# SBUF addresses of the activations moved relative to their weights in every dense product, and the scheduling clock's price of a matmul set to columns plus 17 cycles

## The chip, the cores and the metric

One core of one Trainium2 chip runs the whole program in one launch. The metric is the device time of that launch in microseconds. TensorE (PE in the profile) does the matrix products, VectorE (DVE) and ScalarE (ACT) the elementwise work, GpSimd (POOL) a few fills and some DMA issues, and the SyncE queue (SP) issues most DMAs. The working memory, SBUF, has 128 partitions; a tile has the same byte address in each of them, and an address below is that byte address within a partition.

## The reference, cut to what matters

One layer over 256 latent tokens and 256 context tokens, model width 2048:

```python
z = einsum('bld,dc->blc', h, w_in)            # latent and context
y_s5 = s5_mixer(z[..., :1024], ...)           # complex diagonal state space, scans
y_rw = rwkv_mixer(z_rw mixed with neighbours) # sequential state update, 16 heads, 2 directions
glu = gelu(y_s5) @ s5_glu_w
merged = gate1 * glu_a * sigmoid(glu_b) + gate2 * (y_rw @ rw_proj)
h = h + g1 * (merged @ w_o)
z = modulate(rms_norm(h, norm2_w), sh2, sc2) @ ffn_w13
h = h + g2 * ((silu(z[..., :D_FF]) * z[..., D_FF:]) @ ffn_w2)   # D_FF = 5632
out = rms_norm(h, norm_f)
```

The modulation vectors (shifts, scales and gates) are six blocks of `silu(c) @ ada_w + ada_b`. Everything is fp32.

## The kernel before, in words

**The dense products.** Six weight matrices are multiplied by activations that lie in SBUF as [128, k, tokens]: `win` (activations `hc` for context and `hl` for latent tokens), `glu` (`gl`), `proj` (`yr`), `wo` (`mg`), `w13` (`h2`) and `w2` (`hid`). Weights come from HBM in halves of eight 128x128 tiles (512 KB). ScalarE rounds a half to the reduced fp32 type (`hi`), VectorE makes the rest (`lo` = weight minus `hi`); the activations have been split in the same way into two tiles (names ending in 0 and 1). `Dense.step` then issues, for each 128x128 weight tile, three matmuls into one PSUM accumulator: `hi` with activation 0, `hi` with activation 1, `lo` with activation 0. Each has its own weight load of 128 columns and then moves 256 columns of activations, or 258 in `w13`, where two columns carry the shift. The counts of such matmuls are `win` 1248 with `hc` and 3216 with `hl`, `glu` 768, `proj` 384, `wo` 768, `w13` 4224 and `w2` 2112.

**The order of the work.** Background generators (the S5 and RWKV branches, evacuations, weight preparation) and dense steps are interleaved by `Kernel.drive`. It keeps a rough clock of every engine (`Clock`): `Clock.cost` gives each instruction a price, and `drive` emits a dense step where the picked background step would have to wait on that clock. The order of emission in each engine's queue is fixed by this when the program is built; nothing of it runs on the chip.

**The stages.** A start-up (modulation vectors, norms) runs to about 124 us of the span. Then come the `win` columns used by both token sets (to about 485), the latent-only and gate columns (to about 831) beside S5 and RWKV, the modulation matrix `adaR` as raw fp32 matmuls beside RWKV (about 835 to 1160), `glu` (to 1312), `proj` (to 1370), `wo` (to 1460), `w13` (to 1970) and `w2` (to 2219). The last three have nothing but evacuations and weight preparation beside them, and during `w13` the generator `mod_late`, which makes the last modulation block on VectorE: 32 products of [128, 1024] weights with the row `cbs`, loaded over the GpSimd queue.

**Where tiles lie.** Pools are opened and closed like a stack. A left pool is placed upward from the end of the last left pool, the first of them at 4224; a right pool downward from the start of the last right one. The pools `hr` that hold `hi` and `lo` consist of tiles of 4096 bytes, a weight tile is 512 bytes of one, and one k of the activations is 1024 bytes (1088 in `h2`). So a product's activations stand at one distance from their weights by 512, whichever tile and ring slot is used, and only in `h2` the distance moves with k. Adding up the tile sizes of the pools gives this for the kernel before, all by 512:

| product | activations | weights | distance |
|---|---|---|---|
| win, hc | 0 | 448 | 64 |
| win, hl | 448 | 448 | 0 |
| glu, gl | 128 | 128 | 0 |
| proj, yr | 128 | 448 | 192 |
| wo, mg | 0 | 448 | 64 |
| w13, h2 | 128 + 64 k | 448 | 192 + 64 k |
| w2, hid | 0 | 448 | 64 |

The `glu` weights are in left pools, all other weights in right pools at the top of SBUF.

Of the kernel before, what the change touches and what calls it, by code (L numbers as in the profile page):

```python
# [8 lines left out]
F32 = mybir.dt.float32  # L9
# [8 lines left out]
P = 128  # L18
# [160 lines left out]
class Clock:  # L179
# [41 lines left out]
    def cost(self, eng, op, out, a, k):  # L221
        n = 1
        for d in out.shape[1:]:
            n *= d
        if eng == "tensor":
            if op == "transpose":
                return 0.055 if a[1].shape[0] <= 64 else 0.108
            self.mms += 1
            lhs = k["lhsT"]
            m = lhs.shape[-1]  # L230
            if lhs.dtype == F32R:

                return max(n / 2400 + 0.002, 0.12)

            return (4 * max(n, m) if max(n, m) > 64 else 3 * n) / 2400 + 0.002
        if eng == "vector":
            src = a[1] if len(a) > 1 else k.get("in_")
            if op in ("tensor_copy", "tensor_scalar"):
                return 0.07 + n / (960 if "ps" in src.tensor.name[:2] else 1400)
            if op == "reciprocal":  # L240
                return 0.07 + 6 * n / 960
            return 0.07 + n / 960
        if eng == "scalar":
            c = (0.05 if a[1].tensor.name[:2] == "ps" else 0.1) + n / 1200
            for q in ("bias", "scale"):
                if _aps(k.get(q)) is not None:
                    c += 0.09
            c += self.table_load(a[2])
            return c
        return 0.1 + n / 1000  # L250
# [319 lines left out]
class Kernel:  # L570
# [16 lines left out]
    def pool(self, name, bufs=1, side=None, space=None):  # L587
# [4 lines left out]
            kw["space"] = space  # L592
        return Pool(self.tc.tile_pool(**kw), self.clk, bufs)

    def wide(self, pool, n, tag, name=None, bufs=None):

        return pool.tile([P, -(-n // 16) * 16], F32, tag=tag, name=name or tag, bufs=bufs)[:, 0:n]
# [10 lines left out]
    def run(self):  # L608
        nc, tc, A = self.nc, self.tc, self.A
        es = ExitStack()  # L610
        with es:
            cpool = es.enter_context(self.pool("cpool"))
            dr = es.enter_context(self.pool("dr", space=DRAM))
            self.free_banks, self.held = [], {}
            self.add_banks(es, 4)
            self.cpool = cpool

            edge = es.enter_context(self.pool("edge", side="right"))
            edge.tile([P, 8], F32, tag="edge", name="edge")
            self.cst = self.wide(cpool, NCST, "cst")  # L620
            pp = cpool.tile([P, NPP + 29], F32, tag="pp", name="pp")
            self.pp, self.omu, self.tiny = pp[:, 0:NPP], pp[:, NPP:NPP + 27], pp[:, NPP + 27:]
            nc.gpsimd.dma_start(self.pp, A["pp"])
            nc.gpsimd.dma_start(self.cst, A["cst"])
            self.ada = cpool.tile([P, 96, 2], F32, tag="ada", name="ada")
            self.arow = cpool.tile([P, T], F32, tag="arow", name="arow")
            nc.gpsimd.memset(self.arow, 0.0)
            self.sc = cpool.tile([P, KT, 2], F32, tag="sc", name="sc")
            nc.vector.tensor_scalar(self.omu, self.pc("mu", 0, 27), -1.0, 1.0, op0=ALU.mult, op1=ALU.add)
            self.hka = cpool.tile([P, 2, 8], F32, tag="hka", name="hka")  # L630
            nc.vector.tensor_scalar(self.hka[:, 0], self.pc("ka", 0, 8), 0.5, None, op0=ALU.mult)
            nc.vector.tensor_scalar(self.hka[:, 1], self.pc("ka", 0, 8), -0.5, 1.0, op0=ALU.mult, op1=ALU.add)
            self.hwa = cpool.tile([P, 2, 16], F32, tag="hwa", name="hwa")
            nc.vector.tensor_scalar(self.hwa[:, 0], self.pc("w0", 0, 16), 0.5, None, op0=ALU.mult)
            nc.vector.tensor_scalar(self.hwa[:, 1], self.pc("a0", 0, 16), 0.5, None, op0=ALU.mult)
            nc.vector.memset(self.tiny[:, 0:1], 1e-12)
            nc.vector.memset(self.tiny[:, 1:2], GN_EPS)
            self.A2 = cpool.tile([P, 16], F32, tag="A2", name="A2")
            self.zc = ExitStack()
            self.zcp = zcp = self.zc.enter_context(self.pool("zcp"))  # L640
            self.wad = [zcp.tile([P, 2, T], F32, tag=f"wad{e}", name=f"wad{e}") for e in range(2)]
            self.sgd = zcp.tile([P, T], F32, tag="sgd", name="sgd")
            self.S = [zcp.tile([P, 2, 2, 64], F32, tag=f"S{e}", name=f"S{e}") for e in range(4)]


            self.d_u = dr.tile([1024, 4, 2, 64], F32, tag="d_u", name="d_u")
            self.d_kvr = [dr.tile([P, 512], F32, tag=f"d_kvr{i}", name=f"d_kvr{i}") for i in range(24)]
            self.d_kk = [dr.tile([P, 512], F32, tag=f"d_kk{j}", name=f"d_kk{j}") for j in range(8)]
            self.d_gate = dr.tile([2, P, 16, T], F32, tag="d_gate", name="d_gate")
            self.d_ma = dr.tile([P, 16, T], F32, tag="d_ma", name="d_ma")  # L650
            self.d_win = dr.tile([4, P, 4096], F32, tag="d_win", name="d_win")
            self.d_wout = dr.tile([2, 4, P, 1024], F32, tag="d_wout", name="d_wout")
            self.d_yr = dr.tile([P, 8, T], F32, tag="d_yr", name="d_yr")
            self.d_y = dr.tile([1024, 4, 64], F32, tag="d_y", name="d_y")

            self.flags = Flags(self.clk)
            self.bgs = []
            self.make_jobs()
            self.spawn(self.dense.evacuate(), "evac", self.PRD)
            self.spawn(self.dense.preps(), "prep", self.PRD)  # L660
            self.body()
# [141 lines left out]
    def e_mod(self, q, acc):  # L803


        nc = self.nc
        yield "scalar", acc
        ar = self.arow[:, q % 2 * P:q % 2 * P + P]
        gs = [slice(32 * g, 32 * g + 16) for g in range(4)]
        for g in gs:  # L810
            nc.scalar.activation(ar[g], acc[g], AF.Copy)
        self.dense.drop()
        yield "tensor:1", self.arow
        tp = self.bank([P, 16], f"psmod{q}")
        for g in gs:
            nc.tensor.matmul(tp, lhsT=ar, rhs=self.cs("ident")[:, g], start=(g.start == 0), stop=(g.start == 96))
        f = 32 + 16 * q
        yield "vector", tp
        nc.vector.tensor_tensor(self.ada[:, f:f + 16, 0], tp, self.pc("adab", f, f + 16), op=ALU.add)
        self.free(tp)  # L820
        if q == 2:
            nc.vector.scalar_tensor_tensor(self.A2, self.ada[:, 64:80, 0], 1.0, self.pc("n2", 0, 16), op0=ALU.add, op1=ALU.mult)

    def mod_late(self, pool):

        nc = self.nc
        cbs = pool.tile([P, D], F32, tag="cbs", name="cbs")
        raw = pool.tile([P, 16, 2], F32, tag="adr", name="adr")
        row = self.A["crow"][0:1, :]
        nc.gpsimd.dma_start(cbs, bass.AP(row.tensor, row.offset, [[0, P], [1, D]]))  # L830
        yield "scalar", cbs
# [1 line left out]
        ws = []  # L833

        def load(i):
            if i < 32:
                ws.append(pool.tile([P, 1024], F32, tag="adw", name=f"adg{i}", bufs=2))
                nc.gpsimd.dma_start(ws[i], self.A["adaG"][i // 2][:, 1024 * (i % 2):1024 * (i % 2) + 1024])

        load(0)  # L840
        load(1)
        for i in range(32):
            yield lambda: self.dense.pos >= self.n_wo + 8 + 4 * i
            self.clk.mark = 0.0
            self.after(ws[i])
            yield "vector"
            f, e = i // 2, i % 2
            nc.vector.scalar_tensor_tensor(ws[i], ws[i], 1.0, cbs[:, 1024 * e:1024 * e + 1024], op0=ALU.mult, op1=ALU.mult,
                                           accum_out=raw[:, f, e:e + 1])
            load(i + 2)  # L850
        o = self.ada[:, 80:96, 0]
        nc.vector.tensor_tensor(o, raw[:, :, 0], raw[:, :, 1], op=ALU.add)
        nc.vector.tensor_tensor(o, o, self.pc("adab", 80, 96), op=ALU.add)

# [1433 lines left out]
    def body(self):  # L2288
# [4 lines left out]
        d = self.dense  # L2293
        d.open(0, self.n_win, side="right")
        hl = ExitStack()
        self.hlp = hl.enter_context(self.pool("hlp", side="right"))
        gx = ExitStack()
        self.gp = gx.enter_context(self.pool("gp", side="right"))
# [47 lines left out]
        d.open(self.n_mod, self.n_glu, ahead=1)  # L2346
        d.top_up()
        glx = ExitStack()
        glp = glx.enter_context(self.pool("glp"))
        self.gates = {}  # L2350
        self.spawn(self.load_gl(glp), "gl")
# [38 lines left out]
        self.drive(self.n_proj, drain=False)  # L2390
        tail.close()
        h2p = rest.enter_context(self.pool("h2p", side="right"))
        self.h2 = [h2p.tile([P, KT, T + 16], F32R, tag=f"h2{e}", name=f"h2{e}")[:, :, 0:T + 2] for e in range(2)]
        self.shifts()
        self.drive(self.n_wo, drain=False)
        mgx.close()
# [70 lines left out]
```

## Time and profile before

| | |
|---|---|
| median of 3 runs | 2234.84 us (2229.05 to 2236.33) |
| the profiled execution | 2237.06 us, of which its instructions span 2235.3 us |
| mean granted TensorE clock | 0.944 of full speed |
| HBM read, written | 399.77 MB, 31.98 MB: 193 GB/s over the span |

Times below are microseconds from the first instruction of the profiled execution. PE is the matmuls and PEld the weight loads, which overlap them. A matmul's record lasts longer than the step from one start to the next, since matmuls are pipelined; the step is what the sums use. PEclk is the granted clock as a share of full speed (1.00 is 2.4 GHz, 0.5 is 1.2 GHz). All instructions are recorded by one helper and bear its line, L315, so groups are told apart by their tiles: `psacc` is the accumulator of the dense products (and of `adaR`), and in the tile names of the profile numbers are left out, so that `h` is `h2`.

### The profile page before, as it was taken

What the parts mean: (1) busy time and instruction counts of PE and PEld (TensorE: products, weight loads), DVE (VectorE), ACT (ScalarE), POOL (GpSimd) and SP (SyncE); (2) the same over time, 40 slices, a digit from 0 to 9 for tenths busy, and PEclk for the clock granted to TensorE, in tenths of its full rate; (3) what the DMA queues carried; (4) which work ended last, traced back from release to release, by engine and by line L of the source; (5) the groups of instructions that cost most, each with busy time, mean ns of one, the idle gap of its engine ahead of it and who ended that gap; (6) DMA issues with size and microseconds to landing.
All of it is one profiled execution on the core that took longest, in us unless ns stands there. A gap on an engine that the chain in (4) does not pass through costs nothing.

```text
span 2235.3 us, 48212 instructions
## 1 busy us (share of the span) xinstructions
PE 2091.9 (94%) x19780; PEld 1888.3 (84%) x19780; DVE 1472.7 (66%) x2879; ACT 1103.5 (49%) x1897; POOL 156.7 (7%) x325
## 2 busy tenths in 40 slices
PE   7999999999998998787879879999999999999997
PEld 2279999999897886464648879999999999999997
DVE  2788847899836775787675647656666665554444
ACT  2245455334647767383747535554444444444333
POOL 0001110000101102020011110000000000000000
PEclk9999999999998988586869999999999999999998
DMA  9945556356664445747454386557777775555553
GB/s 366 345 165 185 185 180 207 121 156 211 223 182 158 133 137 168 230 139 231 128 172 142 123 301 206 186 186 232 227 230 230 228 219 185 184 188 185 186 188 132
DMA packets 155980, 434.90 MB, mean 195 GB/s; under 512 B 26480, under 2 KB 39792, under 8 KB 154864
## 3 DMA queue, kind: packets, MB, share of 16 engines
q1 hardware_dynamic: 130192, 360.76, 49.7%
q0 software_dynamic: 18080, 58.48, 7.6%
q10 hardware_dynamic: 7488, 12.59, 1.5%
q8 instruction: 155, 2.54, 0.5%
q14 instruction: 65, 0.53, 0.1%
HBM read 399.77 MB, written 31.98 MB: 193 GB/s over the span
## 4 chain that ended last, share of the span: by engine, by line
PE 68%; DVE 12%; ACT 9%; DMA 8%; issue 3%; SPq 0%; POOL 0%; ACTq 0%; DVEq 0%; POOLq 0%
PE psacc L315 56%; DVE lo L315 4%; DMA w<-in_adaR_dram 4%; PE adacc L315 2%; DMA w<-in_glu_dram 2%; ACT hi L315 1%; PE psyp L315 1%; DVE r L315 1%; PE psbu L315 1%; ACT L315 1%; DMA ad<-in_adaP_dram 1%; ACT AQh L315 1%; PE psss L315 1%; DVE zs L315 1%; ACT SV1h L315 1%
## 5 line engine op out<-in xcount | busy, mean ns | idle before, releaser
L315 DVE TENSOR_TENSOR lo<-w,hi 128x1024 fp32r<-128x1024 f32 x478 | 584.5, 1224 | 412.4 <-ACT hi L315 399.9
L315 ACT ACTIVATE hi<-w 128x1024 fp32r<-128x1024 f32 x478 | 505.9, 1059 | 689.8 <-PE psacc L315 554.6
L315 PE MATMUL psacc<-h,hi 128*128 128x258 f32 x2816 | 507.5, 283 | 1.1 <-ACT hi L315 1.1
L315 PEld LDWEIGHTS psacc<-h,hi 128*128 128x128 f32 x2816 | 436.6, 190 | 1.4 <-ACT hi L315 1.4
L315 PE MATMUL psacc<-hl,hi 128*128 128x256 f32 x2144 | 415.9, 288 | 0.0
L315 PE MATMUL psacc<-h,lo 128*128 128x258 f32 x1408 | 398.1, 283 | 0.8 <-DVE lo L315 0.8
L315 PEld LDWEIGHTS psacc<-hl,hi 128*128 128x128 f32 x2144 | 336.3, 192 | 7.8 <-issue 7.2
L315 PE MATMUL psacc<-hl,lo 128*128 128x256 f32 x1072 | 306.6, 286 | 1.4 <-DVE lo L315 1.4
L315 PEld LDWEIGHTS psacc<-h,lo 128*128 128x128 f32 x1408 | 268.0, 190 | 1.0 <-DVE lo L315 1.0
L315 PE MATMUL psacc<-hid,hi 128*128 128x256 f32 x1408 | 248.8, 280 | 0.0
L315 PEld LDWEIGHTS psacc<-hid,hi 128*128 128x128 f32 x1408 | 214.9, 188 | 0.0
L315 PEld LDWEIGHTS psacc<-hl,lo 128*128 128x128 f32 x1072 | 206.3, 192 | 1.8 <-DVE lo L315 1.8
L315 PE MATMUL psacc<-hid,lo 128*128 128x256 f32 x704 | 196.4, 279 | 0.0
L315 PE MATMUL psacc<-hc,hi 128*128 128x256 f32 x832 | 172.0, 288 | 0.0
L315 PE MATMUL psacc<-w,scp 128*16 128x128 f32 x1536 | 95.8, 357 | 54.1 <-DMA w<-in_adaR_dram 52.8
L315 PEld LDWEIGHTS psacc<-hc,hi 128*128 128x128 f32 x832 | 129.7, 191 | 2.8 <-issue 1.9
L315 PEld LDWEIGHTS psacc<-hid,lo 128*128 128x128 f32 x704 | 131.6, 187 | 0.0
L315 PEld LDWEIGHTS psacc<-w,scp 128*16 128x16 f32 x1536 | 32.2, 106 | 108.9 <-DMA w<-in_adaR_dram 99.5
L315 PE MATMUL psacc<-hc,lo 128*128 128x256 f32 x416 | 116.7, 280 | 0.0
L315 PE MATMUL adacc<-ad,sc 128*2 128x512 f32 x192 | 92.0, 633 | 15.4 <-ACT sc L315 7.8
L315 PE MATMUL psacc<-gl,hi 128*128 128x256 f32 x512 | 98.7, 293 | 1.7 <-ACT hi L315 1.6
L315 PE MATMUL psacc<-mg,hi 128*128 128x256 f32 x512 | 90.5, 280 | 0.0
(371 smaller groups left out, 3398.3 us busy)
## 6 DMA issues: line engine op xcount, KB each, us to landing
w<-in_w_dram SPq DMA_DIRECT2D x264, 512.0 KB, 3.7
w<-in_win_dram SPq DMA_DIRECT2D x134, 512.0 KB, 3.9
w<-in_adaR_dram SPq DMA_DIRECT2D x192, 256.0 KB, 3.4
ad<-in_adaP_dram SPq DMA_DIRECT2D x48, 512.0 KB, 6.4
w<-in_glu_dram SPq DMA_DIRECT2D x32, 512.0 KB, 3.7
adg<-in_adaG_dram POOLq DMA_DIRECT2D x32, 512.0 KB, 5.3
w<-in_wo_dram SPq DMA_DIRECT2D x32, 512.0 KB, 4.2
ad<-in_adaD_dram SPq DMA_DIRECT2D x16, 512.0 KB, 7.3
```

Source lines behind the costliest of these rows:

```text
L315: return f(*a, **k)
```

## The change

Pool sizes and two row lengths change so that tiles move; the price of a dense matmul in the rough clock changes; and `mod_late` works in 64 pieces of 512 columns with three buffers, where it had 32 pieces of 1024 with two. `gap` opens a pool whose one tile nothing uses. `arow`, the row buffer of `e_mod`, had two halves used in turn and has one.

```diff
-                return max(n / 2400 + 0.002, 0.12)
+                return n / 2400 + 0.007
...
+    def gap(self, es, n, side=None):
+        es.enter_context(self.pool("gap", side=side)).tile([P, n], F32, tag="gap", name="gap")
...
-            self.arow = cpool.tile([P, T], F32, tag="arow", name="arow")
+            self.arow = cpool.tile([P, P], F32, tag="arow", name="arow")
...
             self.A2 = cpool.tile([P, 16], F32, tag="A2", name="A2")
+            cpool.tile([P, 32], F32, tag="fill", name="fill")
...
-        ar = self.arow[:, q % 2 * P:q % 2 * P + P]
+        ar = self.arow
...
-        raw = pool.tile([P, 16, 2], F32, tag="adr", name="adr")
+        raw = pool.tile([P, 16, 4], F32, tag="adr", name="adr")
...
-            if i < 32:
-                ws.append(pool.tile([P, 1024], F32, tag="adw", name=f"adg{i}", bufs=2))
-                nc.gpsimd.dma_start(ws[i], self.A["adaG"][i // 2][:, 1024 * (i % 2):1024 * (i % 2) + 1024])
+            if i < 64:
+                ws.append(pool.tile([P, 512], F32, tag="adw", name=f"adg{i}", bufs=3))
+                nc.gpsimd.dma_start(ws[i], self.A["adaG"][i // 4][:, 512 * (i % 4):512 * (i % 4) + 512])
...
-        for i in range(32):
-            yield lambda: self.dense.pos >= self.n_wo + 8 + 4 * i
+        for i in range(64):
+            yield lambda: self.dense.pos >= self.n_wo + 8 + 2 * i
...
+        nc.vector.tensor_tensor(raw[:, :, 0:2], raw[:, :, 0:2], raw[:, :, 2:4], op=ALU.add)
...
         hl = ExitStack()
+        self.gap(hl, 80, "right")
         self.hlp = hl.enter_context(self.pool("hlp", side="right"))
...
         glx = ExitStack()
+        self.gap(glx, 48)
         glp = glx.enter_context(self.pool("glp"))
...
-        self.h2 = [h2p.tile([P, KT, T + 16], F32R, tag=f"h2{e}", name=f"h2{e}")[:, :, 0:T + 2] for e in range(2)]
+        self.h2 = [h2p.tile([P, KT, T + 128], F32R, tag=f"h2{e}", name=f"h2{e}")[:, :, 0:T + 2] for e in range(2)]
```

## Rows read from the trace of the kernel before

**Rows 1.** The page: busy time and share of the span of each engine.
```profile
PE 2091.9 (94%) x19780; PEld 1888.3 (84%) x19780; DVE 1472.7 (66%) x2879; ACT 1103.5 (49%) x1897; POOL 156.7 (7%) x325
```
**Rows 2.** Windows: start:end, length, busy time (instructions) by engine, granted clock, DMA.
```profile
core 0: us, PE busy (x) PEld busy (x) DVE busy (x) ACT busy (x) POOL busy (x), PEclk, DMA share, GB/s
0.00:124.00 124.00, 107.76 (x275) 28.39 (x276) 67.56 (x150) 36.96 (x60) 5.32 (x16) 0.96 0.96 352
124.00:192.00 68.00, 67.99 (x562) 66.91 (x561) 59.39 (x159) 29.16 (x81) 4.93 (x12) 1.00 0.39 131
192.00:410.00 218.00, 216.62 (x1788) 211.81 (x1787) 152.40 (x284) 122.51 (x294) 26.96 (x49) 1.00 0.57 191
410.00:486.00 76.00, 76.00 (x636) 76.00 (x635) 70.52 (x205) 18.84 (x31) 3.25 (x6) 1.00 0.41 125
486.00:770.00 284.00, 269.85 (x2522) 253.45 (x2522) 202.72 (x450) 173.20 (x285) 34.98 (x75) 0.96 0.57 181
...
1000.00:1180.00 180.00, 142.80 (x2082) 97.92 (x2075) 131.55 (x323) 95.85 (x208) 15.65 (x34) 0.73 0.56 180
...
1465.00:1978.00 513.00, 511.09 (x4255) 510.68 (x4254) 328.85 (x512) 228.82 (x271) 15.94 (x30) 1.00 0.67 213
1978.00:2225.00 247.00, 241.60 (x2048) 240.99 (x2046) 115.75 (x118) 97.11 (x105) 0.00 (x0) 0.99 0.53 173
```
**Rows 3.** Chain of waits by line, 192 to 410 us.
```profile
by line: PE psacc L315 66.0%; PE psbu L315 11.5%; PE pskps L315 5.4%; PE pswp L315 3.3%; PE pswtp L315 2.9%; DVE X L315 1.9%; DMA winr<-d_win 1.5%; ACT cb L315 1.4%; issue 1.1%; DVE lo L315 1.0%; DVE zs L315 0.9%; ACT wad L315 0.8%; ACT SB 
```
**Rows 4.** Chain of waits by line, 486 to 600 us.
```profile
by line: DVE lo L315 34.8%; DVE r L315 22.4%; DVE zs L315 14.0%; issue 8.8%; DVE SB L315 3.9%; DVE zo L315 3.8%; DVE psss L315 2.4%; DVE nk L315 2.4%; ACT L315 2.3%; ACT nk L315 1.2%; POOL kt L315 0.9%; ACT hi L315 0.9%; POOL lw L315 0.7%; 
```
**Rows 5.** Chain of waits by line, 1180 to 1320 us.
```profile
by line: DMA w<-in_glu_dram 24.4%; PE psacc L315 14.5%; DMA ma<-d_ma 10.5%; DVE lo L315 10.5%; ACT hi L315 8.4%; issue 5.8%; PE pssph L315 3.5%; ACT AQh L315 3.3%; ACT L315 2.8%; PE psuph L315 2.7%; ACT pR L315 2.3%; PE psy2h L315 2.2%; PE 
```
**Rows 6.** Chain of waits by line, 1465 to 1978 us.
```profile
by line: PE psacc L315 98.2%; issue 0.6%; ACT L315 0.5%; DVE lo L315 0.2%; ACT hi L315 0.2%; ACT nt L315 0.2%; ACT z L315 0.1%; DVE h L315 0.1%; ACT nr L315 0.1%; DVE nv L315 0.1%; ACT cbs L315 0.0%; ACTq L315 0.0%
```
**Rows 7.** Windows, instructions of `yr` alone (proj; clock and DMA as in Rows 2).
```profile
1345.00:1369.00 24.00, 24.00 (x214) 24.00 (x213) 0.00 (x0) 0.00 (x0) 1.00 0.65 213
```
**Rows 8.** Windows, instructions of `hid` alone (w2).
```profile
1980.00:2210.00 230.00, 230.00 (x1955) 230.00 (x1954) 0.00 (x0) 0.00 (x0) 1.00 0.57 185
```
**Rows 9.** Windows, instructions of `mg` alone (wo).
```profile
1372.00:1455.00 83.00, 83.00 (x707) 83.00 (x707) 0.42 (x1) 0.00 (x0) 1.00 0.58 185
```
**Rows 10.** Windows, instructions of `h` alone (w13).
```profile
1480.00:1965.00 485.00, 485.00 (x4054) 485.00 (x4053) 0.00 (x0) 0.00 (x0) 1.00 0.68 216
```
**Rows 11.** Windows, instructions of `psacc` alone, two stretches of win.
```profile
130.00:186.00 56.00, 56.00 (x469) 56.00 (x469) 0.00 (x0) 3.20 (x10) 1.00 0.35 115
415.00:480.00 65.00, 65.00 (x544) 65.00 (x543) 0.00 (x0) 3.84 (x12) 1.00 0.42 126
```
**Rows 12.** Timeline of PE inside w13: start, duration, matmul, number merged.
```profile
1601.85 0.40 PE L315 MATMUL psacc<-h,hi 128*128 128x258 f32 x2
1602.09 0.28 PE L315 MATMUL psacc<-h,lo 128*128 128x258 f32 x1
1602.21 0.41 PE L315 MATMUL psacc<-h,hi 128*128 128x258 f32 x2
1602.46 0.29 PE L315 MATMUL psacc<-h,lo 128*128 128x258 f32 x1
1602.59 0.40 PE L315 MATMUL psacc<-h,hi 128*128 128x258 f32 x2
1602.82 0.28 PE L315 MATMUL psacc<-h,lo 128*128 128x258 f32 x1
1602.94 0.40 PE L315 MATMUL psacc<-h,hi 128*128 128x258 f32 x2
```
**Rows 13.** VectorE groups: shapes, count, busy us, mean ns, idle before.
```profile
L315 DVE SCALAR_TENSOR_TENSOR adg<-adg,cbs 128x1024 f32<-128x1024 f32 x32 | 39.0, 1220 | 0.0
L315 DVE SCALAR_TENSOR_TENSOR zs<-zs,pp,inv 128x512 f32<-128x512 f32 x18 | 13.4, 745 | 0.1
```
**Rows 14.** Windows around a fall of the granted clock.
```profile
600.00:607.00 7.00, 4.96 (x42) 4.76 (x40) 6.02 (x13) 2.62 (x5) 1.43 (x5) 1.00 0.97 313
607.00:614.00 7.00, 5.53 (x68) 4.03 (x70) 1.23 (x1) 5.84 (x7) 0.00 (x0) 0.53 0.50 169
```

More of the change, by code (lines that the diff above doesn't have):

```diff
@@ L835, in load @@
         def load(i):
-            if i < 32:
-                ws.append(pool.tile([P, 1024], F32, tag="adw", name=f"adg{i}", bufs=2))
-                nc.gpsimd.dma_start(ws[i], self.A["adaG"][i // 2][:, 1024 * (i % 2):1024 * (i % 2) + 1024])
-        load(0)
-        load(1)
-        for i in range(32):
-            yield lambda: self.dense.pos >= self.n_wo + 8 + 4 * i
+            if i < 64:
+                ws.append(pool.tile([P, 512], F32, tag="adw", name=f"adg{i}", bufs=3))
+                nc.gpsimd.dma_start(ws[i], self.A["adaG"][i // 4][:, 512 * (i % 4):512 * (i % 4) + 512])
+        for i in range(3):
+            load(i)
+        for i in range(64):
+            yield lambda: self.dense.pos >= self.n_wo + 8 + 2 * i
             self.clk.mark = 0.0
@@ L846, in mod_late @@
             yield "vector"
-            f, e = i // 2, i % 2
-            nc.vector.scalar_tensor_tensor(ws[i], ws[i], 1.0, cbs[:, 1024 * e:1024 * e + 1024], op0=ALU.mult, op1=ALU.mult,
+            f, e = i // 4, i % 4
+            nc.vector.scalar_tensor_tensor(ws[i], ws[i], 1.0, cbs[:, 512 * e:512 * e + 512], op0=ALU.mult, op1=ALU.mult,
                                            accum_out=raw[:, f, e:e + 1])
-            load(i + 2)
+            load(i + 3)
         o = self.ada[:, 80:96, 0]
+        nc.vector.tensor_tensor(raw[:, :, 0:2], raw[:, :, 0:2], raw[:, :, 2:4], op=ALU.add)
         nc.vector.tensor_tensor(o, raw[:, :, 0], raw[:, :, 1], op=ALU.add)
```

## The prediction

> **What bounds the kernel now.** I read the page first: TensorE is busy 94% of the span, no other engine over 66% [rows 1]. A mean over the span hides different limits, so the windows by stage come next [rows 2]. The start-up to 124 us is a DMA stage at 352 GB/s. From 124 to 486 us the PE column is full (360.6 of 362 us), with VectorE close behind it at the end (70.52 of 76 us). From 486 us on PE has gaps, and in 1000 to 1180 us its granted clock is 0.73. From 1465 us to the end of `w2` PE is full again at 0.99 to 1.00 of its clock, while VectorE works 329 of 513 us in `w13`.
>
> Then the chain of waits, stretch by stretch: which link ends last? In `w13` 98.2% of it is the dense accumulator [rows 6], so every nanosecond of a matmul step there is a nanosecond of the end. In 192 to 410 us it is 66.0% `psacc` [rows 3]. In 486 to 600 us it is VectorE (`lo`, `r` and `zs` have 71%) and `psacc` does not appear [rows 4]. Beside `glu` it is DMA and VectorE, with `psacc` at 14.5% [rows 5].
>
> Last, the question that decides this case: how long is one step of a dense matmul in each product? A window that one product fills gives it. Each record is about 0.28 us long [rows 12], so a window counts about 2.4 records that only reach in from its edges; I take them off:
>
> - `proj`, distance 192: 24.00 us / (214 - 2.4) = 113.4 ns [rows 7]
> - `w2`, distance 64: 230 / (1955 - 2.4) = 117.8 ns [rows 8]
> - `wo`, distance 64: 83 / (707 - 2.4) = 117.8 ns [rows 9]
> - `win`, distances 64 and 0 in turn: 56 / (469 - 2.4) and 65 / (544 - 2.4) = 120.0 ns [rows 11]
> - `w13`, all eight distances in turn: 485 / (4054 - 2.4) = 119.7 ns, with 258 columns [rows 10]
>
> All at a granted clock of 1.00, all with PE full, all with a weight load per matmul. The same instruction on the same shapes takes 113.4, 117.8 or 120.0 ns, and what separates the products is the distance from activations to weights by 512. `proj` is the shortest and the only one at a constant 192.
>
> A rule speaks against reading it so. The Trainium skill (SBUF — State Buffer, "Who interferes with whom") gives PE two independent read ports, one for the moving operand and one for weight loads, and says that PE never waits on anyone. By it an address could not matter and the sum below would be nothing. The rows of `proj` and `w2` disagree with that by 4.4 ns a matmul; I go with them, and keep the rule's outcome as a rival.
>
> **The change part by part.** *Does it reach 192 everywhere?* `arow` loses 512 bytes and `fill` adds 128, so every later left pool moves down by 384, which is +128 by 512. `hc`, `mg` and `hid` go from 0 to 128 against weights at 448: 192. `hl` moves down by 320 under its gap, from 448 to 128: 192. `gl` and its weights both move by 128, and the gap of 192 bytes lies between them: 192. `h2` has rows of 384 x 4 = 1536 bytes, three times 512, so k no longer moves it; its pool grows by 32 rows x 448 bytes = 28 x 512, so it still starts at 128: 192 for all k. `yr` stays. So each product should take the step of `proj`: 113.4 ns for 256 columns, and 114.3 for 258 (two more columns at 2.4 GHz are 0.8 ns).
>
> *The gain, product by product*, with counts from the kernel:
>
> - `win` to 486 us: 1248 `hc` + 1248 `hl` = 2496 matmuls x (120.0 - 113.4) = 16.5 us. It counts where `psacc` is the chain: the 144 us before 192 and after 410 whole, the 218 us between by 66% [rows 3], so (144 + 144) / 362 = 80%: 13 us. Bounds 8 to 16.5.
> - `win` after 486 us: 1968 x 6.6 = 13.0 us at most, but VectorE holds the chain [rows 4]: I take 2, nearest to the row that lacks `psacc`. Bounds 0 and 13.
> - `glu`: no window is filled by it; at the 120.0 of `win`, 768 x 6.6 = 5.1 us at most; by 14.5% of the chain [rows 5], 1 us. Bounds 0 and 5.
> - `proj`: 0, its address stays.
> - `wo`: 768 x 4.4 = 3.4 us.
> - `w13`: 4224 x (119.7 - 114.3) = 22.8 us. Bounds below, in the first rival.
> - `w2`: 2112 x 4.4 = 9.3 us.
>
> Together 51.5 us.
>
> *The pieces of `mod_late`.* 32 products of 1220 ns are 39.0 us; a product of 512 columns with three inputs has 745 ns in another group [rows 13], so 64 are at most 47.7: 8.7 us more VectorE work in `w13`, where it would be busy 338 of some 490 us. PE hides it; without that cover it would cost 8.7. The 32 more DMA issues stand on GpSimd, busy 15.94 of 513 us there, with no other issues queued behind them. They are half as large, so the same bytes.
>
> *`arow` in one piece.* The second and third modulation block write it 64 weight pieces after the last one read it; nothing waits.
>
> *The emission order.* The clock's price of a dense matmul falls from 120 to 113.7 ns (114.5 with 258 columns). The rows have 120.0 now and I expect 113.4, so the clock stays as true as it was, but orders around RWKV will differ. The trace of before can't show it. I bound it by the idle time of PE in 486 to 770 us, 284 - 270 = 14 us, to either side, and take 0, because model and machine shift by the same 5%.
>
> *Does something else become late?* In 410 to 486 us PE's wish falls to 76 - 636 x 0.0066 = 71.8 us, and VectorE needs 70.5: it just holds. In `w13` DMA goes from a share of 0.67 to 0.70 and VectorE to 0.69.
>
> The span becomes 2235.3 - 51.5 = 2183.8 us. The profiled execution was 1.8 us longer than its span and 2.2 us above the median of the runs, so against that median I predict 2183 us.
>
> **The rivals.** *A: 258 columns don't take the step of `proj`.* For: in `w13` the rows at distance 192 (k = 0, which counting from the stage's start puts at 1602.21) are the slowest of the eight: 1602.59 - 1602.21 = 0.38 us for three matmuls, against 0.36 at k = 15 before and 0.35 at k = 1 after [rows 12]. Against: these rows come right after a move of the activations by 64 bytes, with whatever lag the queue has, while `proj` stays at 192 for a whole stage and shows no such step. If `w13` keeps 119.7 ns, the time is 2183 + 23 = 2206. If it takes 0.38 / 3 = 126.7 ns, it loses 4224 x 7.0 = 29.6 besides: 2236.
>
> *B: the address is not the cause.* `proj` could be short for another reason (its halves are few), and by the skill's rule of the independent ports the step stays. Then only the emission order moves: about 2235. Against: `wo` and `w2` agree to 0.1 ns at the same distance though one is 768 matmuls beside nothing and the other 2112.
>
> *C: VectorE takes over in `win`.* It is 2% from it in 410 to 486 us and holds the chain after that. The 13 + 2 us there stay away: 2198.
>
> *D, slower: dense work runs out as filler beside RWKV.* In 600 to 607 us PE is busy only 4.96 of 7 us, and the next 7 us are granted 0.53 [rows 14]. Shorter dense steps leave thinner PE activity in 486 to 770 us (now 0.96, 270 us busy). At the 0.73 of 1000 to 1180 us [rows 2] that busy time would grow by 270 x (0.96 / 0.73 - 1) = 85 us: 2268. It decides the sign from 270 x (0.96 / g - 1) = 51.5, a clock of 0.81. Against: the stretch has 0.96 now, and the steps shorten by 5% only.
>
> **How the numbers follow.** Forecast 64%, A 13% (10 at about 2206, 3 near 2236), B 5%, C 14%, D 4%. 0.3%, about 6.7 us, is what a measurement of this kernel can tell. Faster: 64 + 14 + 10 = 88%. Same: B and the end of A, 8%. Slower: 4%. The range: downward, the upper bounds of `win` and `glu` and a lucky order would give 3.5 + 11 + 4 + 14 = 32 us; I go half that way, to 2166. Upward it takes in C and the first of A with part of an order loss: 2212. Left out are B, D, the second of A and the far tails.
>
> **What would show it.** Steps of 113 to 115 ns in windows of `hc`, `hl`, `mg`, `h` and `hid`; `w13` some 23 us and `w2` some 9 us shorter between their first and last matmul; `hc` ending near 472 us. `w13` at 119 ns or above is A; `w2` still at 117.8 is B; VectorE full in 410 to 472 us is C; a granted clock under 0.81 in the stretch of the gates is D. The prediction is wrong in its core if `w2` does not fall below 115 ns, since nothing but an address moves there.

## The result and the profile after

The changed kernel takes 2210.95 us (median of 4 runs, 2202.68 to 2220.10) against 2235.24 us before (2229.05 to 2236.33): a ratio of 0.9895, 95% interval 0.9874 to 0.9916. Faster, as forecast, but by 24 us instead of 52. Its four runs lie 17 us apart, the four of before 7 us; later runs of before lie up to 16 us apart. The profiled execution took 2212.75 us and spans 2211.0 us, 24.3 less than before.

The page of the changed kernel, busy time by engine; TensorE has 32 us less, VectorE 8 and GpSimd 18 us more, ScalarE 4 us less [rows 1]:

```profile
PE 2059.5 (93%) x19780; PEld 1863.4 (84%) x19780; DVE 1480.5 (67%) x2944; ACT 1099.9 (50%) x1896; POOL 174.6 (8%) x357
```

Now the windows that one product fills, of the changed kernel, in this order: `hid` alone (w2), `mg` alone (wo), `h` alone (w13), and `psacc` in two stretches of `win`. They answer to [rows 8 to 11]; columns as there.

```profile
1965.00:2185.00 220.00, 220.00 (x1943) 220.00 (x1943) 0.00 (x0) 0.00 (x0) 1.00 0.59 193
...
1358.00:1437.00 79.00, 79.00 (x699) 79.00 (x699) 0.00 (x0) 0.00 (x0) 1.00 0.60 195
...
1480.00:1950.00 470.00, 470.00 (x3892) 470.00 (x3892) 0.00 (x0) 0.00 (x0) 1.00 0.67 215
...
130.00:186.00 56.00, 56.00 (x477) 56.00 (x477) 0.00 (x0) 3.29 (x10) 1.00 0.33 110
415.00:470.00 55.00, 55.00 (x487) 55.00 (x486) 0.00 (x0) 3.19 (x10) 1.00 0.47 140
```

Length over (count less 2.4) gives the step of a matmul, as in the prediction. `w2` went from 117.8 to 220 / 1940.6 = 113.4 ns and `wo` from 117.8 to 113.4, both to the forecast digit. `win` has 118.0 ns in the first stretch and 113.5 in the second, from 120.0. But `w13` has 470 / 3889.6 = 120.8 ns, where it had 119.7 and should have had 114.3.

Where each stage ends is read from the first and last start of its matmuls. Of the kernel before (count, least/median/most ns, first to last start):

```profile
L315 PE MATMUL psacc<-gl,lo x256: 278/283/416, 1160.2 to 1311.8; 128*128 128x256 f32 x128
...
L315 PE MATMUL psacc<-hc,lo x416: 277/279/283, 125.3 to 484.0; 128*128 128x256 f32 x139
...
L315 PE MATMUL psacc<-hl,lo x1072: 278/283/415, 125.6 to 830.6; 128*128 128x256 f32 x179
...
L315 PE MATMUL psacc<-h,lo x1408: 276/283/580, 1460.1 to 1969.9; 128*128 128x258 f32 x176
...
L315 PE MATMUL psacc<-hid,lo x704: 279/279/279, 1970.2 to 2218.6; 128*128 128x256 f32 x176
```

and of the changed kernel:

```profile
L315 PE MATMUL psacc<-gl,lo x256: 275/277/579, 1136.9 to 1294.4; 128*128 128x256 f32 x128
...
L315 PE MATMUL psacc<-hc,lo x416: 275/279/282, 125.8 to 477.5; 128*128 128x256 f32 x139
...
L315 PE MATMUL psacc<-hl,lo x1072: 275/277/420, 126.1 to 799.3; 128*128 128x256 f32 x179
...
L315 PE MATMUL psacc<-h,lo x1408: 279/283/420, 1440.6 to 1954.9; 128*128 128x258 f32 x176
...
L315 PE MATMUL psacc<-hid,lo x704: 275/277/279, 1955.3 to 2194.3; 128*128 128x256 f32 x176
```

`hc` ends 6.5 us earlier, `hl` 31.3 and `glu` 17.4: between 477 and 799 us the changed kernel wins 25 us more. It gives 14 of it back: 8 between the end of `hl` and the start of `glu`, where DMA of `adaR` has 26.6% of the chain of before (831 to 1159 us) and `psacc` 11.6%, and 6 in `glu`. Part of the work beside them has moved there: ScalarE is busy 211.7 us between `hl` and `glu`, where it had 200.7. From `proj` on, from the same kind of rows (last start to last start, rounded at the end): `wo` lasts 87.0 us instead of 90.5, `w13` 514.7 instead of 510.2, `w2` 239.4 instead of 248.7. So -17.4 to the end of `glu`, +1.3 in `proj`, -3.4, +4.6 and -9.4 make up the 24.3 us.

### The profile page after: what moved, and what is told of

It reads as the page before. It is cut to its first block, busy times and chain, and to the rows that moved or that the text cites. A ratio compares the mean times of both kernels' runs of the same rounds, so it can differ in the third digit from the quotient of the medians.

```text
span 2211.0 us, 48344 instructions
## 1 busy us (share of the span) xinstructions
PE 2059.5 (93%) x19780; PEld 1863.4 (84%) x19780; DVE 1480.5 (67%) x2944; ACT 1099.9 (50%) x1896; POOL 174.6 (8%) x357
## 5 line engine op out<-in xcount | busy, mean ns | idle before, releaser
L315 PE MATMUL psacc<-hl,hi 128*128 128x256 f32 x2144 | 401.0, 283 | 0.0
L315 PEld LDWEIGHTS psacc<-hl,hi 128*128 128x128 f32 x2144 | 328.5, 190 | 8.6 <-issue 8.2
L315 PE MATMUL psacc<-hl,lo 128*128 128x256 f32 x1072 | 300.3, 280 | 3.6 <-DVE lo L315 3.6
L315 PE MATMUL psacc<-hid,hi 128*128 128x256 f32 x1408 | 239.4, 276 | 0.0
L315 PE MATMUL psacc<-w,scp 128*16 128x128 f32 x1536 | 92.0, 359 | 45.2 <-DMA w<-in_adaR_dram 43.9
L315 PE MATMUL psacc<-gl,lo 128*128 128x256 f32 x256 | 75.2, 294 | 13.4 <-DVE lo L315 13.3
```

The source lines that it names most:

```text
L315: return f(*a, **k)
```

## The experiments

The question was why `w13` alone kept its long step. The theory that I took first: the 258 columns (L). Its rivals: another distance would serve 258 columns (D), or something else in `w13` is in the way, such as the longer rows, VectorE or the DMAs (X).

**256 columns in w13.**

```diff
-Job(16, T + 2, act("h2"), ...)
+Job(16, T, lambda k: [(self.h2[0][:, k, 0:T], self.h2[1][:, k, 0:T])], ...)
...
-nc.vector.tensor_copy(b, acc[:, T:T + 1])
+nc.vector.tensor_copy(b, acc[:, T - 1:T])
```

> The changed kernel with w13 moving 256 columns instead of 258: the two shift columns are left out of the product (the bias is read from column 255, so the work after the product is the same in size). Theory L (the length of the moving stream: 258 columns are 8 bytes more than whole pieces of the distance pattern, and that is what takes the gain away): the step falls from 120.8 ns to 113.4 ns, w13 from 515 to about 484 us, the time from 2211 to about 2180 us. Theory X (something else in w13, such as the longer rows of h2, VectorE or the DMAs beside it): the step stays at 119 ns or above and the time within 8 us of 2211.

Measured: 2178.63 us (median of 4 runs: 2176.91, 2178.24, 2179.01 and 2207.33), ratio 0.9786 (0.9716 to 0.9855). Windows of `h` alone and `hid` alone in this kernel:

```profile
1460.00:1915.00 455.00, 455.00 (x4017) 455.00 (x4017) 0.00 (x0) 0.00 (x0) 1.00 0.74 230
...
1930.00:2150.00 220.00, 220.00 (x1943) 220.00 (x1943) 0.00 (x0) 0.00 (x0) 1.00 0.63 194
```

455 / 4014.6 = 113.3 ns. Two columns of 258 are worth 7.5 ns a matmul between these two executions; two columns at 2.4 GHz would be 0.8. The longer rows, VectorE and the DMAs of `w13` are still there, so X falls. One run of four took 29 us more, which no theory had foreseen.

**258 columns at eight distances.** Each row of `h2` is read from a later column, four k to a distance, in two kernels.

```diff
+    H2OFF = (16, 32, 48, 64)      # second kernel: (80, 96, 112, 0)
+    def h2v(self, e, k, a=0, b=T + 2):
+        o = self.H2OFF[k // 4]
+        return self.h2[e][:, k, o + a:o + b]
```

> The changed kernel with the rows of h2 read from a later column, so that the distance of activations to weights in w13 is 256 bytes for k 0 to 3, 320 for k 4 to 7, 384 for k 8 to 11 and 448 for k 12 to 15, all with 258 columns. Theory D (258 columns have their short step at another distance than 192): one of the four groups has a step near 114.3 ns, the others 118 to 127. Theory L (no distance helps a stream of 258 columns): every group keeps 119 to 122 ns.

> As the sweep over 256 to 448, with the distance 0 for k 0 to 3, 64 for k 4 to 7, 128 for k 8 to 11 and 192 for k 12 to 15. Theory D: one group near 114.3 ns if the other sweep has none. Theory L: 119 to 122 ns in all four, with 192 at 120.8 as in the changed kernel.

Measured: 2219.70 and 2208.44 us (one run each). From the starts of the matmuls in each group: 120.3 ns at 256, 118.9 at 320, 120.8 at 384 and 120.9 at 448 in the first; 120.3 at 0, 118.9 at 64, 120.8 at 128 and 120.9 at 192 in the second. None of these eight distances brings 258 columns near 114.3 ns, so D falls for them. Four k are long enough to show a short step, since 256 columns reach 0.34 us for three matmuls within such a group (below); distances that are no multiple of 64 were not tried. Groups 256 apart have the same step here. In the windows the two kernels' `w13` agree to one matmul in 3870, and yet they differ by 11 us. The windows show where 9 of them are, `h` alone and then `hid` alone, first kernel:

```profile
1480.00:1945.00 465.00, 465.00 (x3871) 465.00 (x3870) 0.00 (x0) 0.00 (x0) 1.00 0.69 216
...
1965.00:2190.00 225.00, 225.00 (x1913) 225.00 (x1912) 0.00 (x0) 0.00 (x0) 1.00 0.59 187
```

and second kernel:

```profile
1480.00:1945.00 465.00, 465.00 (x3870) 465.00 (x3869) 0.00 (x0) 0.00 (x0) 1.00 0.69 216
...
1965.00:2180.00 215.00, 215.00 (x1899) 215.00 (x1899) 0.00 (x0) 0.00 (x0) 1.00 0.63 194
```

`w2` runs at 225 / 1910.6 = 117.8 ns in one and 113.4 in the other, at the same addresses and the same distance of 192. That was new: at 192 a stream of 256 columns has two levels.

**The rows of h2 as before.**

```diff
-T + 128], F32R, tag=f"h2{e}"
+T + 16], F32R, tag=f"h2{e}"
```

> The changed kernel with the rows of h2 back at 272 columns, so that the distance in w13 moves with k by 64 bytes as in the kernel before; all else as changed. If the constant distance of 192 is what made w13 slower, w13 goes back from 515 to 510 us and the step from 120.8 to 119.7 ns, the time to about 2206 us. If something else beside w13 did it (the 64 pieces of the late modulation block), w13 stays at 515 us.

Measured: 2215.48 us (one run). Windows of `h` alone and `hid` alone:

```profile
1480.00:1940.00 460.00, 460.00 (x3844) 460.00 (x3844) 0.00 (x0) 0.00 (x0) 1.00 0.69 217
...
1960.00:2190.00 230.00, 230.00 (x1956) 230.00 (x1955) 0.00 (x0) 0.00 (x0) 1.00 0.59 184
```

`w13` goes back to 460 / 3841.6 = 119.7 ns and 508.6 us, as expected. How much of the 1.1 ns the constant 192 costs is not shown, since the changed kernel's own second profile has 120.0 ns there (below). The time went up instead of down; `w2` stands at 117.7 ns here, which is worth 9 us.

The addresses in `w13` are those of the kernel before, but other rows are slow. Before, k = 0, at distance 192, took 0.38 us for three matmuls [rows 12]. Here k = 0 takes 0.36, and 0.38 falls on k = 4, at distance 448. The rows of k = 0, 1, 4 and 5, start first:

```profile
1603.62 0.40 PE L315 MATMUL psacc<-h,hi 128*128 128x258 f32 x2
...
1603.98 0.40 PE L315 MATMUL psacc<-h,hi 128*128 128x258 f32 x2
...
1605.05 0.42 PE L315 MATMUL psacc<-h,hi 128*128 128x258 f32 x2
...
1605.43 0.40 PE L315 MATMUL psacc<-h,hi 128*128 128x258 f32 x2
```

So the slow rows belong to no one distance.

**272 columns.**

```diff
-Job(16, T + 2, act("h2"), ...)
+Job(16, T + 16, act("h2"), ...)
...
```

> The changed kernel with 272 columns moved in w13 (16 copies of the shift column instead of 2), a whole number of 16-column pieces, at the distance of 192. If 258 columns are slow because a piece of 16 columns is broken off, the whole 17 pieces take 272 + 16 columns, 120.0 ns, no more than the 120.8 ns of 258 columns. If a stream longer than 256 pays more for its length alone, the surcharge of 258 (32 columns over its length) gives 304 columns, 126.7 ns, and w13 is 25 us longer than in the changed kernel.

Measured: 2229.17 us (one run); window of `h` alone:

```profile
1480.00:1955.00 475.00, 475.00 (x3854) 475.00 (x3853) 0.00 (x0) 0.00 (x0) 1.00 0.67 211
```

475 / 3851.6 = 123.3 ns, between the two expectations of 120.0 and 126.7. So the broken piece of 16 columns is not the whole cause, and a fixed surcharge isn't either. At 2.4 GHz the steps are 272 cycles for 256 columns, 290 for 258 and 296 for 272. What makes them so is left open.

**The old price with the new addresses, and the new price alone.**

```diff
# the changed kernel with the old price
-return n / 2400 + 0.007
+return max(n / 2400 + 0.002, 0.12)
# the kernel before with the new price: the same two lines, the other way round
```

> The changed kernel with the old price of a dense matmul in the rough clock (120 ns), all addresses as changed. If the gain up to the end of glu comes from the addresses and the price only follows, glu ends within 5 us of the changed kernel's 1294.6 us and the time stays within 5 us of 2211 us unless w2 changes its step. If the emission order brought it, glu ends near the 1312 us of the kernel before.

> The kernel before with the new price of a dense matmul in the rough clock and nothing else: all addresses and the pieces of 1024 columns as before. Theory P (the emission order by itself brings the gain up to the end of glu): glu ends near 1295 us as in the changed kernel, the time is about 2218 us. Theory A+P (order and shorter steps are needed together, since the order with the old price and the new addresses ended glu at 1311 us): with steps of 118 to 120 ns in win, glu ends at 1305 us or later, the time is 2228 us or more.

Measured: 2223.70 us (one run) with the old price; 2228.08 us with the new price alone (10 runs), ratio 0.9971 (0.9956 to 0.9986). Last `glu` start with the old price and the new addresses:

```profile
L315 PE MATMUL psacc<-gl,lo x256: 275/278/581, 1155.0 to 1310.6; 128*128 128x256 f32 x128
```

and with the new price and the old addresses:

```profile
L315 PE MATMUL psacc<-gl,lo x256: 278/283/579, 1150.0 to 1305.7; 128*128 128x256 f32 x128
```

Against 1311.8 us before, the addresses alone bring 1.2 us, the price alone 6.1, and both together 17.4. Most of the gain needs both. A rival is that `win` had its long step in the profile with the old price: 60 / 508.6 = 118.0 ns in 410 to 470 us. The kernel with the old `h2` rows had it there too, 60 / 509.6 = 117.7, with the new price and the same addresses up to `wo`, and its `glu` ends at 1294.0. The window of `psacc` with the old price, then that of the kernel with the old rows and its last `glu` start:

```profile
410.00:470.00 60.00, 60.00 (x511) 60.00 (x511) 0.00 (x0) 3.20 (x10) 1.00 0.47 134
...
410.00:470.00 60.00, 60.00 (x512) 60.00 (x511) 0.00 (x0) 3.72 (x12) 1.00 0.44 128
...
L315 PE MATMUL psacc<-gl,lo x256: 276/276/582, 1134.0 to 1294.0; 128*128 128x256 f32 x128
```

In all eleven profiles with the new addresses and the new price the last `glu` start lies between 1285.4 and 1299.9 us, so the step of `win` does not explain 1310.6. With the old price there is one profile. Why the order holds the gain back is not shown.

**256 columns at four distances.** As the second kernel of the sweep, with 256 columns moved.

> 256 columns in w13 (the two shift columns left out of the product) with the distance 0 for k 0 to 3, 64 for k 4 to 7, 128 for k 8 to 11 and 192 for k 12 to 15. If the distance sets the step of a stream of 256 columns, the groups separate: about 120 ns at 0, 117.8 at 64, 113.4 at 192, and 128 to be seen. If the step is only a matter of how the stream happens to fall in (w2 had 117.8 ns in two executions and 113.3 in three, with the same addresses), all four groups have one step, 113.4 or 117.8 ns.

Measured: 2203.24 us (one run). Timeline of PE in this kernel's `w13`, the rows of the two `hi` matmuls of each k, start first. 1605.33 is k = 12, where the distance becomes 192, and 1606.72 is k = 0 of the next product, at distance 0:

```profile
1605.33 0.40 PE L315 MATMUL psacc<-h,hi 128*128 128x256 f32 x2
...
1605.68 0.40 PE L315 MATMUL psacc<-h,hi 128*128 128x256 f32 x2
...
1606.04 0.39 PE L315 MATMUL psacc<-h,hi 128*128 128x256 f32 x2
...
1606.38 0.39 PE L315 MATMUL psacc<-h,hi 128*128 128x256 f32 x2
...
1606.72 0.39 PE L315 MATMUL psacc<-h,hi 128*128 128x256 f32 x2
...
1607.06 0.40 PE L315 MATMUL psacc<-h,hi 128*128 128x256 f32 x2
...
1607.42 0.40 PE L315 MATMUL psacc<-h,hi 128*128 128x256 f32 x2
...
1607.78 0.40 PE L315 MATMUL psacc<-h,hi 128*128 128x256 f32 x2
```

At 192 three matmuls take 0.35 and 0.36 us, then 0.34 twice. The first k at distance 0 still has 0.34, and then 0.36 comes back. So the step follows where the activations lie, but only after a few matmuls: it has a memory. By group the means are 118.4 ns at 0, 118.1 at 64, 118.6 at 128 and 115.4 at 192, all blurred by these run-ins. The rival that the step is chance alone falls.

Another rival is that the place of the activations counts and not their distance, since here the weights stay at 448 throughout. `glu` settles it, because its weights move too: before, activations and weights both lie at 128; after, they lie at 448 and 256. From the starts of the matmuls in the unbroken stretches of `gl` (39 matmuls or more), before has 119.6 to 120.0 ns, and the changed kernel 113.5 to 113.8, once 117.7. `hl` had its activations at 448 before too, with weights at 448, and 120.0 ns where it runs alone. So activations at 448 go with 120.0 and with 113.5: it is the distance.

**The shift on one matmul of three.**

```diff
 nc.tensor.matmul(a, lhsT=hi[:, cs], rhs=xh, start=(k == 0), stop=False)   # 258 columns in w13
+a, xh = a[:, 0:T], xh[:, 0:T]
-nc.tensor.matmul(a, lhsT=hi[:, cs], rhs=xl, start=False, stop=False)
+nc.tensor.matmul(a, lhsT=hi[:, cs], rhs=xl[:, 0:T], start=False, stop=False)
...
```

> The changed kernel with the shift columns on one matmul of three only: the first (hi with activation 0) moves 258 columns, column 256 the rounded shift and column 257 its rest, the other two move 256; the bias is the sum of the two accumulator columns. The share of the shift that the lo weights have is left out. If each stream pays for its own length, the three take 290 + 272 + 272 columns, 115.9 ns on average, w13 about 21 us shorter than in the changed kernel, the time about 2190 us. If one broken piece upsets the two streams after it too, the step stays at 119 to 121 ns and the time near 2211 us.

Measured: 2206.57 us (4 runs, 2199.68 to 2217.70), ratio 0.9877 (0.9836 to 0.9918), not to be told from the changed kernel. Windows of `h` alone and `mg` alone:

```profile
1480.00:1930.00 450.00, 450.00 (x3823) 450.00 (x3823) 0.00 (x0) 0.00 (x0) 1.00 0.71 221
...
1350.00:1430.00 80.00, 80.00 (x682) 80.00 (x681) 0.00 (x0) 0.00 (x0) 1.00 0.61 188
```

450 / 3820.6 = 117.8 ns, between the two expectations. In this execution `wo`, which the edit leaves alone, had 117.7 ns too, so what the mix costs by itself cannot be read from it.

**The changed kernel again.**

> The changed kernel once more, for a second profile. If the step of a stage is fixed by addresses and length, every stage has the step of the first profile (w13 120.8, w2 113.3 ns). If a stage can settle on one of several levels, w13 lies at 120.0 or 120.8 (both were seen with the same addresses) and w2 at 113.3 or 117.8 ns.

Measured: 2206.65 us (one run). Windows of `h`, `mg` and `hid`, each alone:

```profile
1480.00:1940.00 460.00, 460.00 (x3836) 460.00 (x3835) 0.00 (x0) 0.00 (x0) 1.00 0.67 217
...
1360.00:1435.00 75.00, 75.00 (x639) 75.00 (x638) 0.00 (x0) 0.00 (x0) 1.00 0.58 185
...
1960.00:2180.00 220.00, 220.00 (x1944) 220.00 (x1943) 0.00 (x0) 0.00 (x0) 1.00 0.61 192
```

120.0, 117.8 and 113.3 ns, where the first profile of the very same program had 120.8, 113.4 and 113.4. The level is not fixed by the program. Between their levels `wo`, `w13` and `w2` are worth 3.4, 3.4 (at 0.8 ns) and 9.3 us, 16 us together, which is enough for the 17 us between the runs. That it is their cause is not shown: the other runs have no profile, and 15 runs of the kernel before lie 16 us apart too, though its profile and that of the new price alone have the same steps in these three stages.

**The norm ahead of w13.** What the experiments point to: no shift columns. `h2` is made after the norm, as scaled and shifted activations, and the product is 256 columns wide. Shortened, with `_k` for the part of one k:

```diff
-Job(16, T + 2, act("h2"), ...)
+Job(16, T, act("h2"), ...)
...
+# after the last wo product, for each k:
+nc.vector.scalar_tensor_tensor(t, hres_k, A2_k, rs, op0=ALU.mult, op1=ALU.mult)
+nc.scalar.activation(h2[0]_k, t, AF.Identity, bias=sh_k)
+nc.vector.scalar_tensor_tensor(h2[1]_k, t, sh_k, h2[0]_k, op0=ALU.add, op1=ALU.subtract)
```

> The changed kernel with the norm applied before w13 instead of after it: h2 is x times the scale times the reciprocal root, plus the shift, made after the last wo product, so that no shift columns are needed and w13 moves 256 columns at the distance of 192. Theory L: the step is 113.4 ns (or 117.8, the other level that w2 showed), so w13's matmuls take 31 (or 13) us less than in the changed kernel; ahead of them TensorE waits for the norm and for h2, estimated at 4 + 16 x 0.96 = 19 us less what overlaps. Time about 2195 us at the short level, about 2215 at the long one.

Measured: 2194.19 us (median of 6 runs, 2188.0 to 2225.18). The ratio of 0.9816 (0.9794 to 0.9839) leaves out the run of 2225 us. It beats the kernel before. By this interval it beats the changed kernel too, but the steps below mark the run of 2225 us as this program's own, and with it the mean of the six is 2199.2 us, a ratio of 0.984 whose interval, estimated from the same runs, reaches to about 0.990, into the changed kernel's 0.9874 to 0.9916. So that it beats the changed kernel is likely and not shown. The profile is that of the run of 2225 us; a second execution follows.

> The version with the norm ahead of w13 once more, for a second profile; the first had 117.8 ns in w13 and w2 and 2225 us, while its other runs had a median of 2192 us. If these two stages settle on one of two levels together, this execution has 113.4 ns in both and about 2192 us, or 117.8 in both and about 2220 us. If the level is chosen stage by stage, one of them may differ. If the 2225 us had another cause, the steps stay at 117.8 ns with a time near 2192 us.

Measured: 2200.07 us (one run). Windows of `h` alone and `hid` alone in the first profile:

```profile
1480.00:1950.00 470.00, 470.00 (x3993) 470.00 (x3992) 0.00 (x0) 0.00 (x0) 1.00 0.70 221
...
1970.00:2200.00 230.00, 230.00 (x1956) 230.00 (x1955) 0.00 (x0) 0.00 (x0) 1.00 0.57 184
```

and in the second, followed by the 18 us around the norm, all instructions:

```profile
1480.00:1935.00 455.00, 455.00 (x4017) 455.00 (x4017) 0.00 (x0) 0.00 (x0) 1.00 0.74 229
...
1950.00:2175.00 225.00, 225.00 (x1988) 225.00 (x1986) 0.00 (x0) 0.00 (x0) 1.00 0.61 191
...
1436.00:1454.00 18.00, 8.56 (x67) 7.65 (x65) 9.28 (x15) 11.56 (x16) 0.00 (x0) 0.77 0.46 142
```

117.8 and 117.7 ns in the first, 113.3 and 113.3 in the second. The two stages went together, and (4224 + 2112) x 4.4 ns = 28 us is the size of the 25 us between the two executions. It is also the size of the odd run of the 256-column kernel, which has no profile. Against the long step of 256 columns the two columns of 258 are worth 2 to 3 ns, not 7.5. The price of this version stands in the last row: PE is idle for 9.4 of 18 us at the norm and granted 0.77 of its clock there.

## Why the prediction was wrong in size

**The step that failed is the `w13` term.** The prediction put 4224 x (119.7 - 114.3) = 22.8 us there, on the sentence that each product should take the step of `proj`, with 0.8 ns for two more columns. It measured +4.6 us. The difference of 27.4 us is the size of the whole miss (51.5 forecast, 24.3 in the profile); the others, 1.4 us won to the end of `glu` and 1.3 us lost in `proj`, cancel. Rival A described it and had 13%. The sweep shows that 258 columns have no short step at any of eight distances, and the 256-column kernel that the length is what takes it away. Why two more columns do it stays open. I had read the slow rows at k = 0 [rows 12] as a matter of distance 192 or of the move to it; with the old rows of `h2` they stood at k = 4, so they could tell neither. All the products from which I took the rule move 256 columns; the one with 44% of the forecast gain moves 258, and no row of before had 258 columns at a constant distance.

**The reading of the addresses was right for 256 columns, and its digits were partly luck.** `wo` and `w2` came out at 3.4 and 9.4 us, forecast 3.4 and 9.3. The Trainium skill (SBUF — State Buffer, "Who interferes with whom") gives PE two independent read ports and says that PE never waits on anyone; the section is about engines that get in each other's way. As the prediction read it, that an address could not matter, these runs disagree: the same matmul at the same clock takes 117.8 ns at distance 64 [rows 8] and 113.4 at 192, and rival B falls. But 192 allows 113.4 and 117.8 ns. Of the twelve profiles with the new addresses `wo` has the short step in ten and `w2` in seven; with the long one it gains nothing. `proj` itself, from which the 113.4 was taken, has 29 / 245.6 = 118.1 ns (117.8 from the starts) in the kernel before with the new price, at the same addresses:

```profile
1335.00:1364.00 29.00, 29.00 (x248) 29.00 (x248) 0.00 (x0) 0.00 (x0) 1.00 0.66 215
```

One window of one profile could not show that.

**The early stages came out right for a partly wrong reason.** Forecast 16 us to the end of `glu`, measured 17.4. I had put 13 before 486 us, where 6.5 came (`win` stood at 118.0 ns for part of it; in the second profile, with 113.4 there, `hc` ends at 472.8, near the 472 of the forecast), 2 in the rest of `win`, where 25 came, and 14 of these were then given back. And the emission order, which I set to 0 because "the clock stays as true as it was", was mis-sized: alone it brings 6.1 us to the end of `glu`, and with the old price only 1.2 us of the 17.4 arrive. Rival C did not happen (VectorE 52.88 of 60 us in 410 to 470, while the step there fell to 113.5). Nor did D: the clock of 486 to 770 us was 0.98, from 0.96 [rows 2]; between `hl` and `glu` it was 0.71, from 0.73.

The window rows behind these two, all engines, of the changed kernel:

```profile
410.00:470.00 60.00, 60.00 (x531) 60.00 (x531) 52.88 (x149) 16.46 (x28) 2.70 (x5) 1.00 0.43 128
486.00:770.00 284.00, 271.03 (x2633) 254.91 (x2631) 206.77 (x459) 170.46 (x275) 35.06 (x75) 0.98 0.61 193
```

**The pieces of `mod_late`** cost VectorE 43.9 us in place of 39.0 [rows 13], under the bound of 47.7, and hid behind PE as forecast:

```profile
L315 DVE SCALAR_TENSOR_TENSOR adg<-adg,cbs 128x512 f32<-128x512 f32 x64 | 43.9, 686 | 0.0
```

## What to carry to other kernels

Divide a window that one product fills by its count of matmuls, for every product: the same instruction with different steps is a lead that no busy share shows. Carry such a step over only to a product that is alike in everything the rows vary, the length of the stream above all, and price the rest from both ends, since the largest term deserves the hardest look. A step that was read in one window of one profile may be one of several levels. Where an order is planned from prices, change the price with what it prices; and where runs of one program spread, take a second profile before explaining a few us.

## What was not expected of the hardware

- 256 columns behind a weight load at distance 192 settle at 113.3 or 117.8 ns (272 or 283 cycles at 2.4 GHz) and stay there as long as the matmuls follow one another without a pause, for a whole stage in `wo` and `w2`. Two profiles of one program differ in it: `wo` had 113.4 and 117.8 ns in the changed kernel, `w13` and `w2` 117.8 and 113.3 in the version with the norm first. At distance 64 only 117.8 was seen for whole stages, in two kernels; at distance 0 the stretches of `hl` alone have 119.9 to 120.0. What chooses the level was not found.
- A stage that follows without a pause kept the level of the one before it where both moved 256 columns at 192: `wo`, `w13` and `w2` all at 113.3 in the 256-column kernel, `w13` and `w2` together in both profiles of the last version, and the end of `proj` and `wo` together in all twelve profiles with the new addresses (ten short, two long).
- 258 columns at 192 had 120.0 or 120.8 ns, 272 columns 123.3. In the sweep the steps of 258 columns do not change when the distance changes by 256 bytes. Where the distance moves with k, they do: k = 0 and k = 4 lie 256 bytes apart and take 0.38 and 0.36 us before, 0.36 and 0.38 with the old rows of `h2`.
